# ConvFFN of a hybrid encoder layer: token passes reordered to 768, 768 and 576, feature tiles walked back and forth, operands reloaded in one transfer per product

## The chip, the core and the metric

The kernel runs on one core of a Trainium2 chip, in float32, with matrix operands split into a high and a low half (float32r). The metric is the device time of one execution in microseconds, as the median of several runs.

## What is computed

The kernel is one inference step of one layer for a prompt of 2048 tokens and a sample of 64 tokens. Its first part is token mixing (latent attention and gated linear attention). After it come the output projection with a gated residual, a second norm with modulation, and the gated ConvFFN, and these are what the change touches:

```python
x = x + mods[2][:, None, :] * mixed                 # mixed = concat(o_mla, o_gla) @ w_out
h = _modulate(x, p['g_norm2'], mods[3], mods[4])
a, g = jnp.split(h @ p['w_up'], 2, axis=-1)         # w_up (1024, 2*2816)
a_ext = jnp.concatenate([hist, a], axis=1)
conv = p['b_conv']
for j in range(3):
    conv = conv + p['w_conv'][j] * a_ext[:, j:j + L]
y = (jax.nn.gelu(conv) * g) @ p['w_down']           # w_down (2816, 1024)
return x + mods[5][:, None, :] * y, a_ext[:, L:]    # outputs, new convolution history
```

## The kernel before

**Stages.** Projections, gated linear attention and attention take the first 1431 us. Then 17 output tiles of 128 tokens (the last, tile 16, is the sample with 64) go through `out_tile` (L1050): transposes, 48 products with w_out, residual, norm, transposes, and the eight combinations in `comb` (L1084). The FFN follows from L1228 on.

**The up-product** is a seven-product scheme (Strassen-Winograd) on halves of the model dimension, of features against gates, and of token halves. `PRODUCTS` (L58) lists its seven products m with the combination s of `comb` that each uses. `h2[m]` holds a pair of tiles per product, the high half and the low half of that combination, for all tokens of a pass. Each product is 12 matmuls in three-term split form. An FFN step handles one tile of 128 features f (22 of them) for one token pass; `PASSES` (L55) are tiles 0 to 3 with the sample, 4 to 9, and 10 to 15. Hence 66 steps, numbered n. Each matmul of a product has 288 columns in pass 0 and 384 in passes 1 and 2.

**What a step does** is written out by hand in `slot` (L1253), where `at(t, fn)` puts an operation at a due time and all operations of PE, ACT, DVE and POOL are emitted in the order of their due times (L1512). A step has its seven products, the sums of banks (`keep`, `add_bank`, `sum_kept`), three convolution taps, gelu, the gating and the split of the result u into halves. In the gaps between products 5, 3, 7 and 4 and after them stand the down-products of the step before (`down_tile`, one per token tile, 6 matmuls of 512 columns), each with an addition to its accumulator `acc`. Beside that the step prepares the next step's weights: four block sums on POOL (`block_sum`), seven splits (high half on ACT, low half for 5, 6, 7 and 3 on POOL, for 1, 2 and 4 on DVE). The row weights `wd` are loaded and split in the step that uses them. All loads and stores are issued from SP's queue. Column weights are loaded two steps ahead (`load_next`) into four buffers `fst`.

**The turn** between two passes: tiles 4 to 15 store `comb` to `comb_d` in device memory (L1109), one tensor per tile, 8 KB runs per partition. In the last step of a pass, each product's operands are fetched in three pieces of two transfers (`fetch`, L1413) into four staging buffers `h2st`, then split into `h2` (`piece_hi` on ACT, `piece_lo` on DVE, the last piece on POOL). The down tiles of that step also finish the outputs: `residual` loads the x1 rows into two buffers `xs`, `gate_` multiplies the accumulator by the gate row (POOL for even tiles, DVE for odd ones, DVE for all at the end), `finish_` adds `xs` on DVE and stores y. Each of these is due a few us after its tile's products. At f = 0 an accumulator is copied from PSUM by ACT instead of added.

**The start.** `ffn_start` (L1183) frees the output projection's pools, loads the convolution rows, and at the last tile the column weights of steps 0 and 1 are loaded and those of step 0 summed and split (L1212 to L1225). `comb` has a single buffer.

Of the kernel before, what the change touches and what calls it, by code (L numbers as in the profile page):

```python
# [21 lines left out]
P = 128  # L22
# [32 lines left out]
PASSES = ((0, 4, True), (4, 6, False), (10, 6, False))  # L55
# [6 lines left out]
def kernel(  # L62
# [51 lines left out]
    comb_d = [dr.tile([P, 8, 4, 64], F32, tag=f"combd{t}", name=f"comb_d{t}") for t in range(4, NT)]  # L114
# [933 lines left out]
    gt, wk4, h2 = {}, None, {}  # L1048

    def out_tile(t, n, seq, src, pos0, tok0):  # L1050
# [4 lines left out]
        if t in (0, 4, NT):  # L1055
            gt[seq] = gate_rows(wk, 0, seq, "gate")
# [16 lines left out]
        yield "proj"  # L1073
        x1 = wk.tile([P, D], F32, tag="x1", name="x1", bufs=1)
# [4 lines left out]
        Q.dma_start(x1_d[tok0:tok0 + n], x1[:n])  # L1079
        xn = norm_rows(wk, x1, n)  # L1080
# [23 lines left out]
        if t < 4 or seq:  # L1104
            c0 = 64 * (4 if seq else t)
# [32 lines left out]
    hp = c5.enter_context(tc.tile_pool(name="hp", bufs=1, side="right"))  # L1138
# [7 lines left out]
    def gate_rows(pool, g, s, tag):  # L1146

        o = pool.tile([P, D], F32, tag=tag, name="gate", bufs=1)
# [5 lines left out]
    fw = fcol = hist = None  # L1154
# [7 lines left out]
    def load_cols(c0):  # L1162
        s = fw.tile([P, KD, P], F32, tag="fst", name="fst", bufs=4)
# [19 lines left out]
    def ffn_start():  # L1183
        nonlocal fw, fcol, hist
        c4.close()
        fw = c7.enter_context(tc.tile_pool(name="fw", bufs=1))
        fcol = fw.tile([P, 4, NF], F32, tag="fcol", name="fcol")
        hist = fw.tile([P, 2, NF], F32, tag="hist", name="hist")
        fr = fw.tile([4 * NF, P], F32, tag="sraw", name="fr", bufs=4)
        Q.dma_start(fr[:3 * NF], w_conv.rearrange("j (f p) -> (j f) p", p=P))  # L1190
        Q.dma_start(fr[3 * NF:], b_conv.rearrange("j (f p) -> (j f) p", p=P))
        fh = fw.tile([4 * NF, P], F32, tag="sraw", name="fh", bufs=4)
        Q.dma_start(fh[:2 * NF], state_ffn_conv.rearrange("j (f p) -> (j f) p", p=P))
        yield
# [5 lines left out]
    with ExitStack() as c6:  # L1200
        wk = wk4 = c6.enter_context(tc.tile_pool(name="wk4", bufs=2, side="right"))

        next(outs[0])
        for t in range(len(tiles) + 1):
            g = outs[t] if t < len(tiles) else iter(())
            prev = outs[t - 1] if t else iter(())
# [378 lines left out]
```

## Time and profile before

| | |
|---|---|
| median of 3 runs | 3227.69 us (3224.61 to 3233.64) |
| the profiled execution's own time | 3225.37 us |
| its span, first to last instruction | 3223.0 us |
| TensorE matmul busy | 3037.8 us, 94% of the span |
| weight loads / DVE / ACT / POOL busy | 2649.7 / 2495.6 / 1477.4 / 1430.2 us |
| mean granted TensorE clock | 0.968 of full speed |
| moved by DMA | 295 MB, mean 92 GB/s |

The busy shares are averages over stages with different limits. To read a stage, take the busy time of each engine in a stretch of it: the engine that is busy in the whole stretch sets its length, and where none is, a chain of waits does. The granted clock is 1.00 where TensorE runs at full speed. The chain of waits names, going back from the last instruction, what each step of the way waited for. All stretches in the FFN are cut where a step's first product starts.

### The profile page before, as it was taken

Reading aid. Unit: us, or ns where it says so; the run is one execution under the profiler, and the core shown is the slowest. Engines: PE = TensorE matmul, PEld = TensorE weight load, DVE = VectorE, ACT = ScalarE, POOL = GpSimd, SP = SyncE. Lnnn points to the kernel's source line nnn. Section 1 sums busy time; section 2 is a strip of 40 time slices with the busy share of each in tenths; the row PEclk is TensorE's granted clock in tenths of the full one; section 3 lists DMA queues with packets and bytes.
Section 4 is the critical chain, followed back from the end, with each engine's and each line's share of the span. In section 5 each row is a group of like instructions: output and inputs, shape, how many; then the busy total and the mean of one; then the engine's idle time right before and its main releaser. Section 6 shows DMA issues by size and latency. Waiting matters only on the chain.

```text
span 3223.0 us, 46980 instructions
## 1 busy us (share of the span) xinstructions
PE 3037.8 (94%) x16730; PEld 2649.7 (82%) x16730; DVE 2495.6 (77%) x4640; ACT 1477.4 (46%) x3211; POOL 1430.2 (44%) x1161
## 2 busy tenths in 40 slices
PE   8999999999899999999979999979999998999996
PEld 4999787888668888877858888869999987999995
DVE  4776788777788888865438999977787888778786
ACT  4655433333357777754325444444343443434341
POOL 0222222212232322103248888866666666666661
PEclk9999999999889999999989999989999999999998
DMA  7544521111121211113562322252222234222222
GB/s 255 158 132 121 144 76 59 50 56 43 61 69 48 66 44 54 33 38 125 202 212 74 91 79 82 89 186 66 72 61 78 59 115 144 68 70 65 73 61 85
DMA packets 296410, 295.34 MB, mean 92 GB/s; under 512 B 60727, under 2 KB 239751, under 8 KB 294639
## 3 DMA queue, kind: packets, MB, share of 16 engines
q1 hardware_dynamic: 296175, 292.34, 29.6%
q8 instruction: 131, 2.15, 0.3%
q14 instruction: 104, 0.85, 0.1%
HBM read 223.73 MB, written 68.55 MB: 91 GB/s over the span
## 4 chain that ended last, share of the span: by engine, by line
PE 40%; POOL 7%; DVE 5%; issue 4%; DMA 2%; ACT 1%; SPq 0%; POOLq 0%; ACTq 0%; DVEq 0%
PE bank L1272 19%; PE bank L1448 11%; PE bank L96 6%; POOL sraw L1176 3%; POOL wu L1344 3%; DVE acc L1459 1%; PE bank L876 1%; PE bank L863 1%; DVE wu L1344 1%; DVE acc L1481 1%; DMA xs<-x_d 1%; POOL m L1297 1%; DMA h2st<-comb_d 1%; DVE cv L1330 1%; ACT wu L1391 0%
## 5 line engine op out<-in xcount | busy, mean ns | idle before, releaser
L1272 PE MATMUL bank<-h,wu 128*128 128x384 f32 (+1 forms) x5544 | 960.0, 328 | 66.5 <-ACT m L1291 58.3
L1272 PEld LDWEIGHTS bank<-h,wu 128*128 128x128 f32 x5544 | 922.7, 191 | 103.7 <-ACT m L1291 71.8
L1448 PE MATMUL bank<-wd,u 128*128 128x512 f32 (+1 forms) x2244 | 573.1, 399 | 11.3 <-DVE wd L1344 8.5
L1344 POOL TENSOR_TENSOR wu<-sraw,wu 128x512 fp32r<-128x512 f32 x260 | 376.7, 1449 | 392.3 <-ACT wu L1391 390.9
L1448 PEld LDWEIGHTS bank<-wd,u 128*128 128x128 f32 (+1 forms) x2244 | 411.2, 187 | 99.0 <-DVE wd L1344 9.4
L1459 DVE TENSOR_TENSOR acc<-acc,bank 128x512 f32<-128x512 f32 (+1 forms) x714 | 451.3, 678 | 47.2 <-PE bank L1448 42.8
L96 PE MATMUL bank<-w_g,hs 128*128 128x512 f32 (+4 forms) x1632 | 319.8, 346 | 0.0
L1344 DVE TENSOR_TENSOR wu<-fst,wu 128x512 fp32r<-128x512 f32 x195 | 234.2, 1227 | 96.3 <-ACT wu L1391 95.6
L96 PEld LDWEIGHTS bank<-w_g,hs 128*128 128x128 f32 (+1 forms) x1632 | 249.2, 187 | 33.9 <-issue 2.5
L91 DVE TENSOR_TENSOR pp<-bank,pp 128x512 fp32r<-128x512 f32 (+5 forms) x344 | 196.0, 576 | 37.3 <-ACT pp L88 32.7
L876 PE MATMUL bank<-pp,vv 128*128 128x512 f32 (+5 forms) x688 | 209.8, 391 | 13.0 <-DVE ob L900 6.7
L851 ACT ACTIVATE pr<-bank,mx 128x512 f32<-128x512 f32 (+4 forms) x328 | 204.7, 629 | 30.5 <-DVE mx L844 21.1
L1330 DVE SCALAR_TENSOR_TENSOR cv<-a_sb,fcol,cv 128x768 f32<-128x768 f32 (+1 forms) x132 | 212.0, 1606 | 5.1 <-ACT cv L1326 2.9
L88 ACT CAST pp<-bank 128x512 fp32r<-128x512 f32 (+5 forms) x344 | 170.0, 504 | 97.7 <-PE bank L863 95.2
L839 DVE TENSOR_REDUCE mx<-bank 128x1 f32<-128x512 f32 (+4 forms) x328 | 194.9, 599 | 24.5 <-PE bank L838 18.6
L1391 ACT CAST wu<-sraw 128x512 fp32r<-128x512 f32 x260 | 159.6, 614 | 97.1 <-POOL sraw L1176 59.7
L96 PE MATMUL bank<-w_o,mT 128*128 128x512 f32 (+1 forms) x816 | 199.0, 400 | 3.7 <-ACT mT L88 3.2
L96 PEld LDWEIGHTS bank<-w_o,mT 128*128 128x128 f32 (+1 forms) x816 | 149.8, 187 | 46.6 <-DVE mT L91 6.7
L1297 POOL TENSOR_TENSOR m<-m,m 128x384 f32<-128x384 f32 (+1 forms) x132 | 168.4, 1276 | 42.3 <-ACT m L1291 37.2
L1176 POOL TENSOR_TENSOR sraw<-fst 128x512 f32<-128x512 f32 x132 | 184.9, 1401 | 2.3 <-DMA fst<-w_up 2.3
L863 PE MATMUL bank<-ident,pr 128*128 128x128 f32 (+1 forms) x1112 | 178.0, 275 | 3.3 <-DVE pp L91 2.2
L1326 ACT ACTIVATE cv<-a_sb,fcol 128x768 f32<-128x768 f32 (+1 forms) x66 | 64.7, 981 | 243.0 <-DVE a_sb L1314 237.5
(254 smaller groups left out, 5197.1 us busy)
## 6 DMA issues: line engine op xcount, KB each, us to landing
fst<-w_up SPq DMA_DIRECT2D x132, 512.0 KB
fst<-w_down SPq DMA_DIRECT2D x66, 512.0 KB
x<-x_prompt SPq DMA_DIRECT2D x32, 512.0 KB
ada_w<-w_ada SPq DMA_DIRECT2D x64, 256.0 KB
comb_d<-comb SPq DMA_DIRECT2D x12, 1024.0 KB
h2st<-comb_d SPq DMA_DIRECT2D x84, 128.0 KB
wst<-w_ada SPq DMA_DIRECT2D x16, 512.0 KB
hT_d<-hT SPq DMA_DIRECT2D x16, 512.0 KB
```

The lines of the kernel that those rows point to most:

```text
L91: (lo_eng or V).tensor_tensor(lo, src, hi.bitcast(F32), op=ALU.subtract)
L96: T.matmul(out, a, b, start=first and i == 0, stop=last and i == 2)
L851: S.activation(pr[:qn, :b - a], box["s", i, j][:qn, :b - a], AF.Exp, bias=nb, accum_out=ls[:qn, i, j:j + 1])
L863: T.transpose(pt[:kn, i * qn:(i + 1) * qn], pr[:qn, j * P - a:j * P - a + kn], ident[:qn, :qn])
L876: T.matmul(box["o"][:, cs_], vv[:kn, key0 // P + j, :], pp[i][:kn, cs_], start=j == 0 and i == 0, stop=j == nk - 1 and i == 1)
L1176: G.tensor_tensor(s, x, y, op=op)
L1272: T.matmul(b[:, :cols_], w[m][i][:, k], h2[m][j][:, k, :cols_], start=first and k + i + j == 0, stop=k == 3 and i == 1, skip_group_check=n ...
L1297: G.tensor_tensor(o[a][:, :cols_], o[a][:, :cols_], o[b][:, :cols_], op=ALU.add)
L1330: V.scalar_tensor_tensor(v, o["a"][:, j:j + tot], col(j), v, op0=ALU.mult, op1=ALU.add)
L1344: eng.tensor_tensor(out[1], src, out[0].bitcast(F32), op=ALU.subtract)
L1448: T.matmul(po[c][:rows_], o["u"][a][:, c0:c0 + rows_], o["wd"][b][:, c * 512:(c + 1) * 512], start=a + b == 0, stop=a == 1)
L1459: V.tensor_tensor(x, x, y, op=ALU.add)
```

## The change

- `PASSES` becomes tiles 0 to 5, tiles 6 to 11, and tiles 12 to 15 with the sample: 768, 768 and 576 tokens. Output tiles run in their natural order 0 to 16, tiles 0 to 5 are split into `h2` at once, and 6 to 16 are stored.
- `comb_d` is one tensor per later pass, in the layout of `h2`. A tile's store then consists of 32 runs of 256 bytes per partition.
- The reload at a turn is one transfer per product straight into the low half's tile `h2[m][1]`; the high half is cast from it in two halves by ACT, the low half is subtracted in place in two halves, on POOL for products 5, 6 and 7 and on DVE for the others.
- Pass 1 walks the feature tiles from 21 down to 0, so the first step of a pass has the f of the step before it. That step reuses the column weights `w` (`w_next = w`) and the row weights (`wd_kept`): no loads, sums and splits for it.
- The finals of a turn: the gate multiplication is in halves and on DVE, the final addition on POOL, and their due times are 5.5 us per tile apart, from 1.6 us after the first down tile. In the last step the final addition is on DVE for odd tiles and on POOL for even ones, and due times stay.
- Accumulators are a ring of eight buffers in a pool of their own, opened in step 0.
- `out_tile` has one more `yield`, after the residual. The convolution rows are loaded and transposed at tile 4, step 0's column weights are loaded at tile 13, and after tile 16's residual they are summed and split, before tile 15's last part. Tile 16's norm and combinations are put into FFN step 0, at 0.1 and 7.5 us.
- The pools around the FFN get `reuse_waits="tile"`, by its name a wait per tile for the memory of a closed pool.

```diff
-PASSES = ((0, 4, True), (4, 6, False), (10, 6, False))
+PASSES = ((0, 6, False), (6, 6, False), (12, 4, True))
...
-    comb_d = [dr.tile([P, 8, 4, 64], F32, tag=f"combd{t}", name=f"comb_d{t}") for t in range(4, NT)]
+    comb_d = [dr.tile([P, 8, 4, 64 * nt + 32 * smp], F32, tag=f"combd{t}", name=f"comb_d{t}") for t, nt, smp in PASSES[1:]]
...
         yield "proj"
+        wk = wk4b
...
         Q.dma_start(x1_d[tok0:tok0 + n], x1[:n])
+        yield "res"
         xn = norm_rows(wk, x1, n)
...
-            Q.dma_start(comb_d[t - 4], comb)
+            Q.dma_start(comb_d[p - 1][:, :, :, c0:c0 + hn], comb[:, :, :, :hn])
...
-    otiles = tiles[:4] + tiles[NT:] + tiles[4:NT]
-    outs = [out_tile(*ti) for ti in otiles]
+    outs = [out_tile(*ti) for ti in tiles]
...
-    hp = c5.enter_context(tc.tile_pool(name="hp", bufs=1, side="right"))
+    hp = c5.enter_context(tc.tile_pool(name="hp", bufs=1, side="right", reuse_waits="tile"))
+    fc = c5.enter_context(tc.tile_pool(name="fc", bufs=1, side="right", reuse_waits="tile"))
...
+        if t == 4:
+            conv_rows(w0)
+        if t == len(tiles) - 4:
+            raws = [{"a": load_cols(0, w0, 2), "g": load_cols(FF, w0, 2)}]
+        next(prev, None)
+        next(prev, None)
+        if t == len(tiles) - 1:
+            next(g)
+            c6a.close()
+            c4.close()
+            fw = c7.enter_context(tc.tile_pool(name="fw", bufs=1, reuse_waits="tile"))
+            raws.append({"a": load_cols(P), "g": load_cols(FF + P)})
+            for m in (5, 6, 7, 3):
+                block_sum(raws[0], m)
+            w_f = {}
+            for m, s in PRODUCTS:
+                w_f[m] = two(f"wu{m}_")
+                split(*w_f[m], block(raws[0], m), lo_eng=G if m in (3, 5, 6, 7) else V)
+        next(nxt, None)
+        next(prev, None)
...
-        steps = [(p, f) for p in range(len(PASSES)) for f in range(NF)]
+        steps = [(p, f if p % 2 == 0 else NF - 1 - f) for p in range(len(PASSES)) for f in range(NF)]
...
+            if first_f and n:
+                at(base + 2, rows_kept)
+            else:
+                at(base + 2, rows)
+                at(after + 1.0, rows_hi)
+                at(after + 2.5, lambda: lo(o["wd"], o["sd"], V))
...
+            if raw is None:
+                w_next = w
...
-            if f == NF - 1 and p + 1 < len(PASSES):
+            if last_f and p + 1 < len(PASSES):
+                w1 = 64 * PASSES[p + 1][1] + 32 * PASSES[p + 1][2]
+                there = base
+
+                def fetch(m, s):
+                    moving(m)
+                    Q.dma_start(h2[m][1].bitcast(F32)[:, :, :w1], comb_d[p][:, s])
+
+                def half_hi(m, ks):
+                    S.copy(h2[m][0][:, ks, :w1], h2[m][1].bitcast(F32)[:, ks, :w1])
+
+                def half_lo(m, ks, eng):
+                    h, l = h2[m][0][:, ks, :w1], h2[m][1][:, ks, :w1]
+                    eng.tensor_tensor(l, l.bitcast(F32), h.bitcast(F32), op=ALU.subtract)
+
                 for m, s in PRODUCTS:
...
+                    there = max(there, end[m]) + 3.3
+                    at(end[m] + .1, fetch, m, s)
+                    for i in range(2):
+                        ks, eng = slice(2 * i, 2 * i + 2), G if m in (5, 6, 7) else V
+                        at(there + 1.5 + i, half_hi, m, ks)
+                        at(there + 2.6 + (2.0 if eng is G else 1.2) * i, half_lo, m, ks, eng)
...
+                    if first_f:
+                        acc[i] = ac.tile([P, D], F32, tag="acc", name="acc", bufs=8)
...
+                    late = o.setdefault("late", t) + 5.5 * i + 1.6
...
-                        V.tensor_tensor(a, a, o["xs", i, c][:rows_], op=ALU.add)
+                        (V if last and i % 2 else G).tensor_tensor(a, a, o["xs", i, c][:rows_], op=ALU.add)
...
+                        at(t - 1.5 + c * .5 if last else late - 4 + c, residual, c)
+                        at(t + 1.4 + c * .1 if last else late + 2.5 * c, gate_, c)
+                        at(t + 2.5 + c * .1 if last else late + 1 + 2.5 * c, finish_, c)
...
+        raws += [{} if n % NF else None for n in range(2, len(steps))] + [None] * 2
...
+        at(.1, next, outs[-1])
+        at(7.5, next, outs[-1])
+        at(13.0, open_acc)
```

## Rows read from the trace of the kernel before

**Rows 1.** Timeline of TensorE: start us, us, engine line op tiles xcount [idle before <-releaser]

```profile
1647.34 11.63 PE L96 MATMUL bank<-w_o,mT 128*128 128x512 f32 x48
...
1692.37 6.13 PE L1272 MATMUL bank<-h,wu 128*128 128x288 f32 x24 [13.52 <-ACT m L1291]
...
2099.70 3.25 PE L1272 MATMUL bank<-h,wu 128*128 128x288 f32 x12 [9.80 <-ACT m L1291]
```

**Rows 2.** Windows, by stage: stretch, its us, each engine's busy us, clock, DMA

```profile
core 0: us, PE busy (x) PEld busy (x) DVE busy (x) ACT busy (x) POOL busy (x), PEclk, DMA share, GB/s
1593.30:1606.43 13.13, 13.13 (x67) 10.66 (x65) 5.89 (x12) 3.87 (x8) 3.87 (x5) 1.00 0.54 201
1658.97:1704.85 45.88, 20.32 (x102) 18.35 (x101) 14.59 (x29) 15.16 (x30) 25.80 (x25) 0.67 0.56 185
1704.85:1725.22 20.37, 18.71 (x116) 16.46 (x115) 17.29 (x23) 13.62 (x28) 18.71 (x17) 1.00 0.27 78
1968.00:1986.84 18.84, 18.63 (x117) 16.46 (x116) 18.70 (x28) 8.30 (x17) 15.84 (x13) 1.00 0.29 85
2081.93:2179.81 97.88, 73.48 (x350) 65.62 (x348) 78.12 (x96) 43.27 (x78) 69.67 (x48) 0.86 0.53 164
2226.30:2249.55 23.25, 23.25 (x122) 21.60 (x120) 18.50 (x26) 9.30 (x16) 14.32 (x12) 1.00 0.23 68
2621.49:2719.41 97.92, 78.39 (x362) 70.04 (x360) 86.29 (x95) 43.66 (x77) 67.95 (x43) 0.90 0.52 164
3161.09:3184.30 23.21, 23.21 (x121) 21.41 (x119) 14.61 (x23) 5.55 (x9) 3.28 (x3) 1.00 0.00 1
3184.30:3223.00 38.70, 9.64 (x39) 6.67 (x38) 25.87 (x36) 1.60 (x2) 0.00 (x0) 0.71 0.48 150
```

**Rows 3.** Chain of waits: start us, us, what; issue to landing where DMA

```profile
1432.33 2.01 DMA mix_d<-ob
...
1674.10 8.81 DMA comb_d<-comb
...
1687.92 3.82 DMA comb_d<-comb
...
3192.12 1.34 DMA conv_prompt<-ob
...
3196.61 3.92 DMA xs<-x_d
```

**Rows 4.** Timeline: one width on DVE without and with POOL beside, and on POOL

```profile
1692.86 0.69 DVE L1344 TENSOR_TENSOR wu<-fst,wu 128x512 fp32r<-128x512 f32 x1 [0.73 <-ACT wu L1391]
...
1937.00 1.77 DVE L1344 TENSOR_TENSOR wu<-fst,wu 128x512 fp32r<-128x512 f32 x1
...
2232.56 1.29 POOL L1176 TENSOR_TENSOR sraw<-fst 128x512 f32<-128x512 f32 x1
```

**Rows 5.** Timeline of FFN steps: undisturbed operations, and the first down-product of a step

```profile
2182.56 1.22 DVE L1344 TENSOR_TENSOR wd<-fst,wd 128x1024 fp32r<-128x1024 f32 x1
...
2188.29 1.55 PE L1448 MATMUL bank<-wd,u 128*128 128x512 f32 x6
...
3175.66 2.07 DVE L1330 SCALAR_TENSOR_TENSOR cv<-a_sb,fcol,cv 128x768 f32<-128x768 f32 x2
...
3177.36 2.35 POOL L1297 TENSOR_TENSOR m<-m,m 128x384 f32<-128x384 f32 x2 [17.65 <-ACT m L1291]
...
3179.79 1.01 POOL L1337 TENSOR_TENSOR cv<-cv,m 128x384 f32<-128x384 f32 x1
...
3184.12 0.83 ACT L1341 CAST u<-cv 128x768 fp32r<-128x768 f32 x1 [5.51 <-PE bank L1448]
...
3185.51 0.95 DVE L1348 TENSOR_TENSOR u<-cv,u 128x768 fp32r<-128x768 f32 x1
```

**Rows 6.** Timeline of two output tiles: a comb store's issue, the next tile's first write

```profile
1601.56 0.32 SPq L1109 DMA_DIRECT2D comb_d<-comb  x1
...
1608.94 0.40 DVE L1098 TENSOR_SCALAR comb<-bank,mod_a,mod_b 128x128 f32<-128x128 f32 x1
```

More of the change, by code (lines that the diff above doesn't have):

```diff
@@ L1144, with gate_rows @@
         moving(m)
-    def gate_rows(pool, g, s, tag):
-        o = pool.tile([P, D], F32, tag=tag, name="gate", bufs=1)
+    def gate_rows(pool, g, s, tag, bufs=1):
+        o = pool.tile([P, D], F32, tag=tag, name="gate", bufs=bufs)
         Q.dma_start(o, gate_d[g, s:s + 1].partition_broadcast(P))
@@ L1198, in ffn_start @@
             V.tensor_copy(dst.rearrange("p j f -> p (j f)"), pt[:, :n])
[L1200 to L1206, printed above, removed]
-            nxt = outs[t + 1] if t + 1 < len(tiles) else iter(())
-            next(nxt, None)
-            next(g, None)
-            if t == 0:
-                next(g)
-            if t == len(tiles) - 1:
-                start = ffn_start()
-                next(start)
-                raws = [{"a": load_cols(i * P), "g": load_cols(FF + i * P)} for i in range(2)]
-                for m in (5, 6, 7, 3):
-                    block_sum(raws[0], m)
-            next(prev, None)
-            next(nxt, None)
-            if t == len(tiles):
-                run(start)
-                w_f = {}
-                for m, s in PRODUCTS:
-                    w_f[m] = two(f"wu{m}_")
-                    split(*w_f[m], block(raws[0], m), lo_eng=G if m in (3, 5, 6, 7) else V)
-            next(prev, None)
@@ L1228 @@
-    with ExitStack() as c8:
-        wk = c8.enter_context(tc.tile_pool(name="wk5", bufs=1))
+    c6, c6a = ctx.enter_context(ExitStack()), ctx.enter_context(ExitStack())
+    w0 = c6.enter_context(tc.tile_pool(name="w0", bufs=1, side="right", reuse_waits="tile"))
+    wk4b = c6.enter_context(tc.tile_pool(name="wk4b", bufs=1, side="right", reuse_waits="tile"))
+    wk = wk4 = c6a.enter_context(tc.tile_pool(name="wk4", bufs=2, side="right", reuse_waits="tile"))
+    next(outs[0])
+    for t in range(len(tiles)):
+        g = outs[t]
+        prev = outs[t - 1] if t else iter(())
+        nxt = outs[t + 1] if t + 1 < len(tiles) else iter(())
+        next(nxt, None)
+        next(g, None)
+        if t == 0:
+            next(g)
[6 more added lines that the diff above has]
+        if t == len(tiles) - 1:
+            next(g)
+            c6a.close()
[8 more added lines that the diff above has]
+                split(*w_f[m], block(raws[0], m), lo_eng=G if m in (3, 5, 6, 7) else V)
+        next(nxt, None)
+        next(prev, None)
@@ L1399, in slot @@
             if raw_next is not None:
-                g_ = (f + 2) % NF
+                g_ = steps[n + 2][1]
                 def load_next(k):
@@ L1441, in products @@
                 def products():
-                    if f == 0 and i == 0:
-                        acc.clear()
-                        acc.extend(wk.tile([P, D], F32, tag=f"acc{j}", name=f"acc{j}") for j in range(nt + smp))
+                    if first_f:
+                        acc[i] = ac.tile([P, D], F32, tag="acc", name="acc", bufs=8)
                     o["po", i] = po = [bank(), bank()]
```

96 lines of the change are left out of this document (40 added, 56 removed).

## The prediction

> **What bounds the kernel now.** I read the chain of waits first, then cut the span where it changes character, at the starts of FFN steps. A step is one feature tile f of one pass: 84 up-products, among them the down-products of the step before. Step numbers n run 0 to 65; a turn is the three steps around a change of pass, and E is the end of the last output projection, at 1658.97 us [rows 1]. The stretches in [rows 2] add up to the time from E to the end:
>
> - start, steps 0 and 1: 45.88 + 20.37 = 66.3
> - steps 2 to 20, small pass: from 1725.22 to 2081.93, 356.7 (18.8 each)
> - turn 1, steps 21 to 23: 97.9
> - steps 24 to 42, large pass: 441.7 (23.25 each)
> - turn 2, steps 43 to 45: 97.9
> - steps 46 to 65: from 2719.41 to 3184.30, 464.9
> - tail: 38.7
>
> The sum is 1564.0, and 1658.97 + 1564.0 = 3223.0, the span. A large step is TensorE's own: PE is busy in all of its 23.25 us, DVE in 18.50, POOL in 14.32. A small step is not: DVE is busy 18.70 of 18.84. The output projection tiles too are PE's, 13.13 of 13.13. So time can only be won at the start, the two turns and the tail, where PE is busy 20.3 of 45.9, 73.5 and 78.4 of 97.9, and 9.6 of 38.7 [rows 2]; there the granted clock also falls to 0.67, 0.86, 0.90 and 0.71.
>
> What holds PE there? At the start PE is idle 13.52 us [rows 1]: the last tile's `comb` waits for its single buffer, whose store was issued at 1674.10 behind the FFN's loads and took 8.81 us instead of 3.82 [rows 3]. ACT's copies for step 0 queue behind that `comb`. In the turns PE idles up to 9.80 us for ACT copies [rows 1] that queue behind reloaded pieces. Under that lies a second bound. A 128x512 DVE op with both inputs in SBUF takes 0.69 us with POOL idle and 1.77 beside POOL work; the same width on POOL takes 1.29 [rows 4]. If such DVE work and all POOL work are added at undisturbed lengths [rows 4, 5], a large step has on DVE 2.07 (taps) + 3x0.69 + 1.22 + 0.95 + 0.48 (half of 0.95, estimated) = 6.8, and on POOL 8x1.29 + 2.35 + 1.01 = 13.7, together 20.5. Scaling its token-wide terms by 578/768 gives 18.8 for a small step, which takes 18.84. Turn 2 has 3x20.5, reload splits 14x0.69 + 7x1.29 = 18.7, gates 6x1.29 + 3x1.22 = 11.4 and finals 12x0.69 = 8.3: 99.8, and takes 97.9. Turn 1 gives 95.5 in the same way, and takes 97.9. So I use this side-by-side sum as the turn's limit. It is a regularity of these four stretches, not a law.
>
> **The change part by part.** *Start.* Tile order becomes 0 to 16, pass 0 needs tiles 0 to 5 only, and E does not move: tile count and widths are the same. Step 0's column weights are loaded three tiles early, and their sums and splits go into space that w_o releases row by row if the tile-wise reuse does what its name says; the conv rows move to tile 4. That puts 4 sums and 4 POOL splits (8x1.29 = 10.3) beside a projection during which POOL is busy only 3.87 of 13.13 [rows 2]. Splits that are not done by E lie under the first products. The last tile's norm is cut in two and moved into step 0, so nothing of it stands before product 1. On PE's path I count 1 us of transposes for tile 15, 2 for a first split that comes late, 14.8 for the up-products (by columns, 84x384 of the 84x384 + 36x512 that make up 23.25) and 0.6 for tile 16's transposes: 18.4, taken as 19. In step 1 POOL is still late: 10.3 for step 0, eight `comb` sums of half that width or less (about 5) and a step's own 13.7 make 29 from about E - 7, and the first down-product of step 1 is due 8.5 us into it, at E + 27.5. I add 4 for that. Together 19 + 23.25 + 4 = 46. The bounds are 40 (no wait) and 74 (today's 66.3 plus 8 because both steps are now large).
>
> *comb store.* Eleven tiles store `comb` in 256-byte pieces, 4096 of them, instead of 128 long ones. The `comb` buffer is single: the store is issued 7.38 us before the next tile's first write (1601.56 to 1608.94) [rows 6]. 22 KB took 1.34 us and 128 KB in 256-byte pieces 2.01 [rows 3], so 8 x 0.67 + 1.34 = 6.7 us is my estimate; it just fits, and I count 0. The lower bound is 3.82, today's long store; the upper 8x2.01 = 16.1. The Trainium skill (DMA: Bandwidth & Descriptors, Specifications) speaks against this edit: it puts line rate at pieces of 512 bytes or more, with a read-modify-write below. By the row the sum stays; by the page the store is slower than a long one by a factor that it doesn't give, which is the slower rival below.
>
> *Reload.* 42 transfers per turn become 7 of 768 KB (576 KB at turn 2), written straight into the low halves' tile. At the rate of the 1 MB store (3.82, of it 1.34 fixed) [rows 3] 768 KB take 3.2, and the code spaces them at 3.3 us, each behind its product. By the code's due times each split is done 7 us or more before its product in the next step, so a transfer may take about 4 us without harm. Behind a late one ACT queues with its bank copies (in order, as today); 14 half casts at 0.83 [rows 5] are 11.6 on an ACT that is busy 9.30 of 23.25. On SP the fetches stand before the column loads for two steps later, which have a step to spare.
>
> *Turn 1* is now three large steps: 61.4. It loses one step's column preparation (8x1.29 + 3x0.69 = 12.4) and one row split (1.2). Reload splits are 8x0.95 on DVE and 6x1.94 (1.5x1.29) on POOL = 19.2, half a us more than today. Gates are all on DVE (12x0.69 = 8.3), and finals move from DVE to POOL, 12x1.29 = 15.5 instead of 8.3. Sum 90.8 against PE's 3x23.25 = 69.8: 21 over. Of these 4.5 are free, since a step's last split ends at 2183.78 and its first down-product starts at 2188.29 [rows 5], and the next step repays 23.25 - 20.5 = 2.8. I take 14: turn 1 = 83.8. Bounds for the excess: 3 (the spread finals fill idle port time) and 28, today's.
>
> *Turn 2* is one large and two small steps: 20.5 + 2x18.8 - 12.4 - 1.2 + 8x0.71 + 6x1.45 + 8.3 + 15.5 = 82.6, against 23.25 + 2x18.84 and one more down tile (6x0.232 in the code) = 62.3. Of 20 over, 4.5 are free; a small step repays nothing. POOL now waits for `xs` (load 3.92 [rows 3] + 1.29 in each of two buffers, tiles 5.5 apart: just enough), for which I add 1.5. Excess 17, bounds 5 and 35: turn 2 = 79.3.
>
> *Steady steps.* 19 + 19 large at 23.25 are 883.5, 20 small at 18.84 are 376.8. The small pass has a two-column copy from `halo` in place of a memset, not counted.
>
> *Tail.* Ten loads through two buffers, a pair per tile (3.92 + 0.69 each), become eight: -4.6; POOL's even tiles cost 3 x 0.6 more. 38.7 - 3.2 = 35.5; bounds 33 and 40 (a gate row waits in SP's queue).
>
> **Sum.** 46 + 441.7 + 83.8 + 441.7 + 79.3 + 376.8 + 35.5 = 1504.8, against 1564.0: -59. The profiled execution took 3225.4 (span 3223.0) and would take 3166; the median of the runs is 2.3 above the profiled one, so 3168.
>
> **The rivals.** *Turns stay as long as today*: a reload slower than 4 us stalls ACT in order, or POOL waiting for `xs` stalls the sums behind it. For it: the store that took 8.81 among other loads [rows 3]. Against: 7 transfers need no staging buffer. Excess 28 and 35 instead of 14 and 17: 3168 + 32 = 3200. *The start stays*: the new pool waits for all of w_o, or POOL's backlog holds products 6 and 5. Then 74 instead of 46: 3196. *The port sum doesn't hold when work is spread*: excess 3 and 5, start 42: about 3141. *Slower*: the 256-byte store paces the output projection. From a landing of 7.38 us on, each further us delays the next `comb`, nine times (tiles 6 to 15). At 16.1 a tile takes 8.7 more: 78 in all, 3246. The page named above points this way. It beats the gains from a landing of 14 us, which the 2.01 row at its worst reading allows. *The change doesn't do what it says*: kept weights still wait for a reload, and the turns gain nothing; that falls together with the first rival.
>
> **How the numbers follow.** Forecast 0.57 (3155 to 3182); turns stay 0.11; start stays 0.12; port sum fails 0.12; slow store 0.06; none of these, within noise of today 0.02. 0.3% is about what a measurement of this kernel tells from no change, 10 us: faster means below 3218. Faster 0.90, same 0.04 (half-slow stores, or both gains lost), slower 0.06. The range runs from the port rival to the two stay rivals, 3138 to 3202.
>
> **What would show it.** Right: PE idle under 5 us after E; step 1 starting near E + 19; DVE two-input ops at 1.8 us and POOL near full in the turns; small steps at 18.8 at the end. Wrong: `comb` waiting for its DMA in the output tiles, ACT waiting for `comb_d` reloads, turns at 70 (the port sum is no limit) or at 98.

## The result, and the profile after

The changed kernel takes 3176.32 us (median of 4, 3170.42 to 3178.98), the kernel before in the same comparison 3228.95 (median of 4, 3224.61 to 3233.64): a ratio of 0.9834, 95% interval 0.9814 to 0.9854. The prediction was 3168 with a range of 3138 to 3202. The total is 8 us off. Several of its terms missed by more, in both directions.

Windows by stage of the kernel after (columns as in [rows 2]): output tiles, step 0, step 1, steps 2 to 20, turn 1 (steps 21 to 23), step 24, turn 2 (steps 43 to 45), step 46, the small steps 47 to 65 without the last one's end, one small step, and the tail.

```profile
1439.62:1664.15 224.53, 223.18 (x1078) 177.39 (x1078) 113.01 (x202) 77.62 (x172) 76.55 (x98) 1.00 0.59 163
1664.15:1701.34 37.19, 21.44 (x101) 19.54 (x100) 21.79 (x24) 13.15 (x26) 23.71 (x23) 0.77 0.57 139
1701.34:1724.96 23.62, 23.38 (x122) 21.46 (x121) 13.62 (x16) 15.18 (x28) 20.98 (x15) 1.00 0.32 99
1724.96:2165.00 440.04, 440.04 (x2282) 409.24 (x2280) 349.73 (x473) 177.96 (x288) 271.41 (x208) 1.00 0.24 69
2165.00:2248.07 83.07, 74.50 (x362) 67.06 (x360) 75.69 (x79) 36.70 (x61) 63.87 (x37) 0.96 0.49 163
2248.07:2275.58 27.51, 23.71 (x122) 21.39 (x120) 22.62 (x26) 10.80 (x20) 25.37 (x20) 1.00 0.37 113
...
2693.06:2770.43 77.37, 67.04 (x355) 60.26 (x354) 71.30 (x87) 33.10 (x62) 58.48 (x40) 0.91 0.51 154
2770.43:2793.92 23.49, 20.06 (x116) 17.72 (x114) 20.15 (x27) 9.46 (x19) 22.70 (x19) 0.93 0.51 162
2793.92:3139.80 345.88, 345.88 (x2167) 314.12 (x2165) 338.48 (x513) 159.08 (x298) 279.99 (x220) 1.00 0.28 81
...
2921.37:2939.57 18.20, 18.20 (x115) 16.54 (x114) 18.06 (x28) 8.57 (x16) 15.40 (x13) 1.00 0.29 88
...
3139.80:3173.60 33.80, 8.18 (x33) 5.22 (x32) 19.83 (x30) 1.53 (x2) 8.48 (x6) 0.72 0.42 126
```

Against [rows 2]: step 0 takes 37.2 instead of 45.9, at a granted clock of 0.77 instead of 0.67; the two turns of 97.9 are 83.1 and 77.4, but steps 24 and 46 now take 27.5 and 23.5, more than the steps after them; and a small step takes 18.20 with PE busy in all of it, where before it took 18.84 with PE waiting. Term by term, in us:

| stretch | predicted | measured | difference |
|---|---|---|---|
| start to the end of the output projection | 1658.97 | 1664.15 | +5.2 |
| steps 0 and 1 | 46 | 60.8 | +14.8 |
| steps 2 to 20 | 441.7 | 440.0 | -1.7 |
| turn 1 | 83.8 | 83.1 | -0.7 |
| steps 24 to 42 | 441.7 | 445.0 | +3.3 |
| turn 2 | 79.3 | 77.4 | -1.9 |
| steps 46 to 65 | 376.8 | 369.4 | -7.4 |
| tail | 35.5 | 33.8 | -1.7 |

They add up to 3173.7, the span of the profiled execution (3173.6 us, its own time 3175.5), 9.9 above the predicted sum.

**The first 1440 us are the same code and scatter.** The first transpose of the output tiles came at 1431.7 in the kernel before and at 1439.6 after. In the three profiled executions that have the old code behind that point it came at 1431.7, 1437.6 and 1442.1, in the eleven that have the new code, the experiments among them, at 1436.5 to 1446.5. So 8 us of difference there prove nothing about the change. From that transpose on, the profiled kernel before took 3223.0 - 1431.7 = 1791.3 and the one after 1734.0, 57.3 less, against 59 predicted. For the same reason the runs below are compared by stretches that begin with an FFN step, not by their totals.

**The stall that stayed.** Timeline of the kernel after in step 0 (start us, us, engine line op tiles [idle before <-releaser]):

```profile
1671.80 7.52 DVE L261 TENSOR_SCALAR xn<-x,r 64x1024 f32<-64x1024 f32 x1
...
1680.41 1.18 POOL L1105 TENSOR_TENSOR comb<-comb 128x256 f32<-128x256 f32 x1
...
1681.62 11.34 SPq L1112 DMA_DIRECT2D comb_d<-comb  x2
...
1688.23 0.34 DVE L1100 TENSOR_SCALAR comb<-bank,mod_a,mod_b 128x64 f32<-128x64 f32 x1 [6.09 <-DMA comb_d<-comb]
...
1690.89 0.47 ACT L1306 COPY m<-bank 128x384 f32<-128x384 f32 x1
...
1691.41 7.15 PE L1287 MATMUL bank<-h,wu 128*128 128x384 f32 x24 [11.26 <-ACT m L1306]
```

This is the mechanism of [rows 1, 3] again. Tile 15's last `comb` sum ends at 1681.6 on a POOL that is full with step 0's and step 1's sums and splits; only then is its store issued; tile 16's first write of the same buffer waits for it on DVE until 1688.2; ACT's writes alternate with DVE's; and ACT's copy of a product of step 0 (L1306) comes behind them on ACT, at 1690.9. PE waits 11.26 us, 2.3 less than the 13.52 of before. Of the eleven `comb` stores it is the only one that anything waits for, as the view of line 1112 says:

```profile
who waited for it (us, times):
  DVE comb L1100: 6.1, 1
```

### The profile page after: what moved, and what is told of

Read it like the earlier page. It is cut to its first block, busy times and chain, and to the rows that moved or that the text cites. A ratio compares the mean times of both kernels' runs of the same rounds, so it can differ in the third digit from the quotient of the medians.

```text
span 3173.6 us, 46762 instructions
## 1 busy us (share of the span) xinstructions
PE 3028.5 (95%) x16730; PEld 2650.4 (84%) x16730; DVE 2479.6 (78%) x4617; ACT 1472.2 (46%) x3188; POOL 1439.5 (45%) x1170
## 5 line engine op out<-in xcount | busy, mean ns | idle before, releaser
L1359 POOL TENSOR_TENSOR wu<-sraw,wu 128x512 fp32r<-128x512 f32 x252 | 365.4, 1450 | 347.0 <-ACT wu L1415 347.0
L1359 DVE TENSOR_TENSOR wu<-fst,wu 128x512 fp32r<-128x512 f32 x189 | 215.6, 1166 | 93.6 <-ACT wu L1415 92.0
L839 DVE TENSOR_REDUCE mx<-bank 128x1 f32<-128x512 f32 (+4 forms) x328 | 194.9, 599 | 24.4 <-PE bank L838 18.4
L1415 ACT CAST wu<-sraw 128x512 fp32r<-128x512 f32 x252 | 154.9, 615 | 80.9 <-PE bank L1287 47.3
L863 PEld LDWEIGHTS bank<-ident,pr 128*128 128x128 f32 (+1 forms) x1112 | 135.9, 141 | 39.9 <-DVE pp L91 9.3
```

Source lines behind the costliest of these rows:

```text
L839: V.reduce_max(mx[:qn, c:c + 1], po[:qn, :b - a], axis=AX.X)
L863: T.transpose(pt[:kn, i * qn:(i + 1) * qn], pr[:qn, j * P - a:j * P - a + kn], ident[:qn, :qn])
L1359: eng.tensor_tensor(out[1], src, out[0].bitcast(F32), op=ALU.subtract)
```

## Experiments

Times of steps run from a step's first up-product to the next step's. The total of a single execution includes the scatter above, so the text reads stretches. These scatter too: in the four executions that share the code of the turns (the kernel after, e1, e5 and e10) steps 21 to 24 take 110.3 to 110.7 us and steps 43 to 47 take 117.9 to 119.1.

### The start: is it the queue or POOL's backlog?

**e1_late16**

```diff
-        at(7.5, next, outs[-1])
-        at(13.0, open_acc)
+        at(22.0, next, outs[-1])
+        at(27.0, open_acc)
```

> Edit: the last output tile's comb part moves from 7.5 to 22 us into step 0 by the due times, and the opening of the accumulators' space from 13 to 27. Queue theory: the 11.3 us in which PE waited for ACT's copy of product 1 (step 0 took 36.6) came from ACT and DVE standing in order at the last tile's comb writes, which wait for the store of the tile before. Then PE's hole after the first products goes, step 0 falls to 24 to 28, steps 0 and 1 together from 60.8 after the end of the output projection to 48 to 53, and the whole by 8 to 12 us. Rival, POOL's backlog: POOL is busy without a gap from 1674.1 to 1683.3 with step 0's sums and splits, and these hold products 6, 5 and 7 whatever comb does; then step 0 stays at 33 or more. Second rival, the hole only moves: the comb writes stand in the queue ahead of step 1's copies instead, and step 1 grows from 23.6 by 5 or more.

Measured: step 0 took 23.8 instead of 36.6, step 1 27.7 instead of 23.6, together 51.5 instead of 60.2 (52.1 instead of 60.8 from the end of the output projection). Windows of steps 0 and 1, and TensorE's timeline:

```profile
1667.87:1691.64 23.77, 18.45 (x95) 16.53 (x93) 20.18 (x19) 11.92 (x22) 20.83 (x18) 0.93 0.63 164
1691.64:1719.33 27.69, 25.08 (x123) 23.14 (x121) 14.00 (x20) 16.41 (x32) 23.62 (x20) 0.94 0.48 126
```

```profile
1669.01 2.03 PE L1287 MATMUL bank<-h,wu 128*128 128x384 f32 x10 [0.55 <-DVE wu L91]
...
1672.98 0.62 PE L1287 MATMUL bank<-h,wu 128*128 128x384 f32 x2 [1.94 <-ACT wu L88]
...
1683.11 4.49 PE L1287 MATMUL bank<-h,wu 128*128 128x384 f32 x24 [0.98 <-ACT m L1306]
...
1698.75 6.03 PE L1287 MATMUL bank<-h,wu 128*128 128x384 f32 x24 [2.61 <-ACT m L1306]
```

The 11.26 us hole became 0.98, though POOL is fuller than before (20.83 of 23.77, where it was 23.71 of 37.19). So the queue was the cause and POOL's backlog alone was not. The edit also moves the opening of the accumulators' space, but the wait that went is the one that the trace puts down to the `comb` writes. A part of the second rival holds too: these writes now stand ahead of step 1's copies and cost 2.61 there. The net is 8.7 us.

### The turns: is the side-by-side sum a limit?

With a large step behind turn 1 and two small ones behind turn 2 the prediction's side-by-side sum is 90.8 + 20.5 = 111.3 and 82.6 + 2 x 18.8 = 120.2; measured are 110.6 (steps 21 to 24) and 119.1 (steps 43 to 47). For the whole it fits. If it were a limit, every edit of the work would move the turns by its own length.

**e2_finals_dve**

```diff
-(V if last and i % 2 else G).tensor_tensor(a, a, o["xs", i, c][:rows_], op=ALU.add)
+(V if not last or i % 2 else G).tensor_tensor(a, a, o["xs", i, c][:rows_], op=ALU.add)
```

> Edit: in the two turns the additions of the finals (12 of 128x512 in turn 1, 12 in turn 2) go back from POOL to DVE; nothing else moves. Side-by-side sum (the prediction's tool): an addition costs 0.69 on DVE instead of 1.29 on POOL, so 12 x 0.6 = 7.2 us come off each turn: turn 1 with step 24 from 110.6 to about 103.4, turn 2 with step 46 from 100.9 to about 93.7. Rival, DVE's own queue is the bound: DVE is busy in 75.7 of turn 1's 83.1 us already; with 12 more operations of 0.69 to 1.77 it would need 84 to 97, so the turns stay or grow by up to 14. Rival, neither: unchanged within 1 us.

**e3_lo_dve**

```diff
-ks, eng = slice(2 * i, 2 * i + 2), G if m in (5, 6, 7) else V
+ks, eng = slice(2 * i, 2 * i + 2), V
```

> Edit: all 14 low halves of the reloaded operand on DVE; so far 6 of them per turn (blocks 5, 6, 7; 128x768) are POOL's. Side-by-side sum: 0.95 on DVE instead of 1.85 to 1.94 on POOL, so 6 x 0.95 = 5.7 us off turn 1 (110.6 with step 24 to 105) and 6 x 0.7 = 4 off turn 2 (100.9 with step 46 to 97). Rival, DVE's own queue: POOL's six lie beside other work and DVE gets six more in the step before the pass change, ahead of the taps; the turns grow by 3 to 9. Rival, neither: unchanged within 1 us.

**e4_reload**

```diff
-raws += [{} if n % NF else None for n in range(2, len(steps))] + [None] * 2
+raws += [{} for n in range(2, len(steps))] + [None] * 2
...
-            if first_f and n:
-                at(base + 2, rows_kept)
-            else:
-                at(base + 2, rows)
+            at(base + 2, rows)
```

> Edit: at the first step of a pass the column and row operands are loaded, summed and split again, as in every other step, instead of being kept; the passes still walk back and forth. Side-by-side sum: each turn gets 4 sums and 4 low halves on POOL at 1.28, 3 low halves on DVE at 0.69 and one row split at 1.22 back, 13.6 us together: turn 1 with step 24 from 110.6 to about 124, turn 2 with step 46 from 100.9 to about 114, the whole plus 27. Rival, the turns are held by something else (the order in which splits, taps and finals queue, or the transfers): the turns grow by 5 or less each, though DVE's and POOL's busy times grow by 13 and more.

**e7_nofinals**

```diff
-V.tensor_tensor(a, a, o["gate", i][:rows_, cc], op=ALU.mult)
+if last:
+    V.tensor_tensor(a, a, o["gate", i][:rows_, cc], op=ALU.mult)
...
-(V if last and i % 2 else G).tensor_tensor(a, a, o["xs", i, c][:rows_], op=ALU.add)
+if last:
+    (V if i % 2 else G).tensor_tensor(a, a, o["xs", i, c][:rows_], op=ALU.add)
```

> Left out: in the two turns the multiplication by the gate (12 of 128x512 on DVE each) and the addition of the residual (12 on POOL each); loads and stores stay, so the rows of the first two passes are the raw sums. Side-by-side sum: 12 x 0.69 + 12 x 1.29 = 23.8 us of work goes from each turn, more than the excess over PE's time (17.8 and 21.6): turn 1 with step 24 falls from 110.6 to PE's 4 x 23.2 = 93, steps 43 to 47 from 119.1 to 98 to 100. Rival, work costs only part of its length in a turn, as the operand preparation did when it was put back (5.4 and 5.9 us instead of 13.6): the turns fall by 9 to 10 and an excess of 8 to 12 stays, which the reload then owns.

**e8_nolo**

```diff
-at(there + 2.6 + (2.0 if eng is G else 1.2) * i, half_lo, m, ks, eng)
```

> Left out: the low halves of the reloaded operand in both turns (8 operations of 128x768 on DVE, 6 on POOL per turn, 19.2 us at undisturbed lengths); the transfers and the high halves on ACT stay, so the products of the last two passes are off. Without the finals, step 22 still took 29.96 instead of 23.2 and step 44 27.76 instead of about 19.8, so about 7 to 8 us of each turn's excess lie in the first step after the pass change. Theory, the splits' work on DVE and POOL owns them: step 22 falls to 24 to 26, turn 1 with step 24 from 110.6 to 101 to 104, steps 43 to 47 from 119.1 to 110 to 113. Rival, the transfers or ACT's casts own them: step 22 stays at 29 or more and the turns stay within 2 us.

**e9_nospread**

```diff
-at(t - 1.5 + c * .5 if last else late - 4 + c, residual, c)
-at(t + 1.4 + c * .1 if last else late + 2.5 * c, gate_, c)
-at(t + 2.5 + c * .1 if last else late + 1 + 2.5 * c, finish_, c)
+at(t - 1.5 + c * .5, residual, c)
+at(t + 1.4 + c * .1, gate_, c)
+at(t + (2.5 if last else 4) + c * .1, finish_, c)
```

> Edit: in the turns the finals get the due times they had in the kernel before (residual 1.5 us before a tile's last down-product, gate 1.4 after it, addition 4 after it) instead of one tile each 5.5 us; the engines stay as they are (gate on DVE, addition on POOL). Side-by-side sum: the same work in the same turn, so turn 1 with step 24 stays at 110.6 and steps 43 to 47 at 119.1, within 2 us. Rival, spreading is a gain of its own: the gates and additions crowd into the step after the pass change ahead of step work, DVE and POOL hold ACT's and PE's banks, and each turn grows by 5 to 10. Rival, spreading costs: the additions were late only because they wait for their due time, and each turn shrinks by 2 to 5.

Measured, in us, beside what the sum makes of each edit (where PE's own time is longer, 4 x 23.2 = 92.8 and 62.3 + 2 x 18.2 = 98.7, that stands). The sum's entries for e3, e8 and turn 2 use the prediction's lengths, 0.95 and 1.94 for a large and 0.71 and 1.45 for a small half:

| kernel | steps 21 to 24: sum | measured | steps 43 to 47: sum | measured |
|---|---|---|---|---|
| after | 111.3 | 110.6 | 120.2 | 119.1 |
| e2, additions on DVE | 104.1 | 114.5 | 113.0 | 120.1 |
| e3, low halves on DVE | 105.4 | 112.1 | 115.8 | 120.5 |
| e4, operands loaded again | 124.9 | 115.9 | 133.8 | 125.0 |
| e7, no gates and additions | 92.8 | 99.8 | 98.7 | 105.6 |
| e8, no low halves | 92.8 | 102.0 | 105.8 | 113.0 |
| e9, finals not spread | 111.3 | 118.4 | 120.2 | 127.3 |

The sum misses all six edits. Putting 13.6 us of work back (e4) costs 5.4 and 5.9; taking 23.8 out (e7) gains 10.8 and 13.5; moving work from POOL to the engine where it is shorter (e2, e3) loses 1.0 to 4.0 where 4.4 to 7.2 should be gained (of these losses only e2's 4.0 in turn 1 is far above the scatter; the gains are missing in all four); and moving no work at all (e9) costs 7.8 and 8.2. What stands instead is read from the steps. Windows of steps 22 and 23 of the kernel after, of step 23 in e2, of steps 22 and 23 in e7 and in e8, and of step 23 in e9:

```profile
2189.49:2219.99 30.50, 25.80 (x122) 22.78 (x120) 30.43 (x31) 11.82 (x19) 27.61 (x16) 0.94 0.22 70
2219.99:2248.07 28.08, 25.26 (x122) 22.81 (x120) 27.21 (x26) 12.19 (x24) 26.38 (x17) 0.94 0.53 171
```

```profile
2223.78:2259.23 35.45, 25.71 (x121) 23.07 (x120) 31.58 (x39) 13.24 (x25) 18.49 (x12) 0.90 0.52 163
```

```profile
2186.47:2216.44 29.97, 25.81 (x122) 22.79 (x121) 29.31 (x32) 12.04 (x20) 27.59 (x16) 0.94 0.31 99
2216.44:2239.59 23.15, 23.15 (x121) 21.53 (x120) 11.22 (x16) 13.37 (x25) 14.05 (x12) 1.00 0.31 101
```

```profile
2190.89:2214.08 23.19, 23.19 (x121) 21.56 (x120) 17.98 (x23) 11.81 (x19) 14.26 (x11) 1.00 0.29 92
2214.08:2241.78 27.70, 23.73 (x121) 21.40 (x120) 26.79 (x26) 12.24 (x24) 26.14 (x16) 1.00 0.57 173
```

```profile
2222.03:2262.41 40.38, 28.82 (x121) 25.91 (x120) 25.48 (x28) 13.24 (x25) 33.09 (x24) 0.79 0.51 156
```

Step 22 belongs to the reload: DVE is busy in 30.43 of its 30.50 us, and without the low halves (e8) the step takes PE's 23.19 with DVE at 17.98. Part of DVE's busy time may be POOL's doing: single low halves of 128x768 take DVE 1.76 to 2.40 us in this turn beside POOL's work, where an operation of that size takes 0.95 undisturbed [rows 5]. e8 drops the halves of both engines, so their shares are not separated. Steps 23 and 24 belong to the finals: without them (e7) both take 23.16, and step 22 stays at 29.97. The two shares, 10.8 for the finals and 8.6 for the low halves, together are a little more than turn 1's excess of 17.8 over PE's time. An edit counts only until its step falls to PE's 23.2; that is why e7 and e8 gain less than the work they drop. Part of what e4 adds lies in step 21, which has idle time: its step 21 takes 25.1, only 0.6 more than without. e3 gives the full DVE of step 22 six more low halves and makes that step 32.31, against 30.39 to 31.70 in the five executions that share it (the kernel after, e1, e5, e10 and e11). e2 loses in step 23.

In e2's step 23 (35.45) and e9's (40.38) no engine is full: DVE 31.58 and 25.48, POOL 18.49 and 33.09. A chain of waits holds them. It starts at a load of `xs`, first in e2, then in e9:

```profile
2246.89 0.69 DVE L1505 TENSOR_TENSOR acc<-acc,xs 128x512 f32<-128x512 f32 x1 [3.36 <-DMA xs<-x_d]
...
2248.14 1.03 ACT L1341 ACTIVATE cv<-a_sb,fcol 128x768 f32<-128x768 f32 x1 [10.77 <-DVE a_sb L1329]
...
2251.07 4.10 PE L1287 MATMUL bank<-h,wu 128*128 128x384 f32 x12 [7.57 <-ACT m L1306]
```

```profile
2244.84 1.29 POOL L1505 TENSOR_TENSOR acc<-acc,xs 128x512 f32<-128x512 f32 x1 [4.58 <-DMA xs<-x_d]
...
2252.84 0.62 ACT L1415 CAST wu<-sraw 128x512 fp32r<-128x512 f32 x1 [6.58 <-POOL sraw L1181]
...
2253.89 4.21 PE L1287 MATMUL bank<-h,wu 128*128 128x384 f32 x12 [5.00 <-ACT m L1306]
```

An addition waits for its rows, which come through two buffers. Behind it on the same engine stands work of the step: `a_sb` on DVE in e2, the weight sums on POOL in e9. ACT waits for that work, and PE for ACT's copy of a product. In the kernel after, POOL waits only 0.2 us for `xs` in all of turn 1. So the trace gives a reason why spreading pays: the rows have come when the addition is due. The prediction's first rival had named this wait. No run gives `xs` more buffers in a turn, so it is read from the traces and not tested.

**e11_mix** asks whether POOL's share of the excess can be taken away alone: it is e10_tail (below) with the additions of the last two tiles of a turn on DVE.

```diff
-(V if last and i % 2 else G).tensor_tensor(a, a, o["xs", i, c][:rows_], op=ALU.add)
+(V if (i % 2 if last else i > 3) else G).tensor_tensor(a, a, o["xs", i, c][:rows_], op=ALU.add)
```

> Edit: e10_tail, and in the turns the additions of tiles 4 and 5 (4 of 12) on DVE, the other 8 on POOL. All 12 on DVE made step 24 5 us shorter than in the changed kernel (23.1 instead of 27.5) and step 23 7 us longer (35.5 instead of 28.1). Theory: the excess of steps 24 and 46 is POOL's (busy 25.4 of 27.5 and 22.7 of 23.5), that of the steps before it DVE's; taking 5 us from POOL's end alone gives step 24 back 3 to 5 us and step 46 1 to 3 at no cost to step 23: 5 us under e10_tail. Rival, DVE's queue: each addition delays the accumulation that PE's banks wait for; steps 23 or 24 grow as much as POOL gains, within 2 us of e10_tail.

Measured: 3160.71 us, ratio to the kernel before 0.9768 (0.9749 to 0.9787), the same as e10_tail. Step 24 falls to 23.2 from e10's 25.9, step 23 grows to 34.7 from 28.5; steps 21 to 24 take 112.2 against 110.7. The rival's outcome holds: what POOL's end gains is lost a step earlier. DVE is not full there (29.51 of 34.69); as in e2 its additions wait for `xs`, 3.30 and 1.78 us, and PE then waits 6.59 for ACT.

### The small steps: one state or two?

**e5_kick**

```diff
-        G.tensor_tensor(s, x, y, op=op)
+        for _ in range(1 + (extra.get(now[0], 0) if n in (7, 3) else 0)):
+            G.tensor_tensor(s, x, y, op=op)      # extra = {51: 1, 55: 2, 60: 4}
```

> Edit: in three steps of the last pass POOL computes two of the four weight sums again, once each in step 51 (2 operations of 1.28 us more), twice in step 55 (4 more), four times in step 60 (8 more); the values don't change. The last pass of the changed kernel runs at 18.21 us a step (PE busy in all of it), the small steps of the kernel before at 18.84 (DVE busy 18.70). Two-state theory: both are steady states of the same work, told apart by how far POOL lags DVE when DVE reaches the row split; a kick of 2.6 to 10 us pushes the step over, and after at least one of the kicks the steps stay at 18.8. One-state theory: POOL is busy only 15.4 of 18.2 and DVE 18.06 of 18.21, so a kick costs its own excess once and the steps are back at 18.21 two to five steps later; then the 18.84 of the kernel before comes from something in its code.

Measured: step 52 took 18.90, step 55 21.53 and step 60 29.01; each step behind them was back at 18.2. By this run alone the changed kernel has one state.

**e6_relief** (an edit of the kernel before)

```diff
-at(late, lambda m=m, g=g: lo(w_next[m], block(raw, m), G if g else V))
+if n == 9 and g or n == 15 and m != 4:
+    at(late, lambda m=m: S.copy(w_next[m][1], block(raw, m)))
+else:
+    at(late, lambda m=m, g=g: lo(w_next[m], block(raw, m), G if g else V))
```

> The kernel before, with part of the computation replaced: in step 9 the four low halves of weight blocks that POOL computes, and in step 15 those four and two of DVE's three, are written by ACT as plain copies (wrong values; 0.62 us each on ACT). POOL so gains 4 x 1.3 us in step 9, POOL 4 x 1.3 and DVE 2 x 0.7 to 1.8 in step 15. Two-state theory: after one of the two the small steps run at 18.2 instead of 18.84 to the end of the pass, 5 to 11 steps, so the pass is 3 to 7 us shorter. One-state theory: steps are back at 18.8 within two steps; 18.84 is what that code takes.

Measured: steps 4 to 8 at 18.83, step 9 18.24, steps 10 to 16 at 18.09 to 18.17, step 17 18.73, then 18.8 again. The first edit throws the code into the shorter step, and shortly after the second it is back. Whether the shorter one decays by itself is left open by this run, so the second edit was taken out.

**e12_relief9**

```diff
-if n == 9 and g or n == 15 and m != 4:
+if n == 9 and g:
```

> The kernel before, with the four low halves that POOL computes in step 9 written by ACT as plain copies (wrong values), and nothing else: the edit of step 15 that e6_relief had beside it is left away. There steps 10 to 16 took 18.17 us with POOL's first weight sum 0.1 us ahead of the step's first product, and from step 17 on, after the second edit, 18.84 again with that sum 1.55 us into the step. Two-state theory: each state holds itself, and it was the edit of step 15 that threw the code back; now all of steps 10 to 20 take 18.17, 7.4 us less for the eleven. Rival, the faster state decays by itself: from step 16 or 17 on the steps take 18.8 again.

Measured: all of steps 10 to 20 take 18.17. Windows of step 8 and step 14, then POOL's and DVE's timelines in the same two steps:

```profile
1846.40:1865.24 18.84, 18.37 (x115) 16.34 (x114) 18.70 (x28) 8.25 (x16) 15.85 (x13) 1.00 0.29 84
1956.19:1974.36 18.17, 18.17 (x116) 16.48 (x114) 18.03 (x28) 8.58 (x16) 15.44 (x13) 1.00 0.30 88
```

```profile
1847.97 1.30 POOL L1176 TENSOR_TENSOR sraw<-fst 128x512 f32<-128x512 f32 x1
1849.35 1.76 POOL L1176 TENSOR_TENSOR sraw<-sraw,fst 128x512 f32<-128x512 f32 x1
...
1956.08 1.30 POOL L1176 TENSOR_TENSOR sraw<-fst 128x512 f32<-128x512 f32 x1
1957.46 1.30 POOL L1176 TENSOR_TENSOR sraw<-sraw,fst 128x512 f32<-128x512 f32 x1
...
1849.88 2.32 DVE L1344 TENSOR_TENSOR wd<-fst,wd 128x1024 fp32r<-128x1024 f32 x1
1852.12 1.77 DVE L1344 TENSOR_TENSOR wu<-fst,wu 128x512 fp32r<-128x512 f32 x1
...
1959.36 1.21 DVE L1344 TENSOR_TENSOR wd<-fst,wd 128x1024 fp32r<-128x1024 f32 x1
1960.50 0.67 DVE L1344 TENSOR_TENSOR wu<-fst,wu 128x512 fp32r<-128x512 f32 x1
```

The same instructions, steady in two ways. In the longer step POOL's first sum starts 1.6 us behind the step's first product (1847.97 against 1846.40), its second lies beside DVE's row split, and that split takes 2.32. In the shorter one the first sum starts 0.1 us ahead (1956.08 against 1956.19), both are done before the row split, and that takes 1.21 and the next split 0.67 instead of 1.77. The work that POOL was spared lay in one step; eleven steps ran shorter. The shorter order does not hold from every start: in the three executions with the old code step 2 takes 18.17 and step 3 18.5 to 18.6, and then come steps of 18.8. The last pass of the changed kernel has the shorter order from step 47 on (in the step shown above POOL's first sum starts at 2921.23, 0.14 ahead of the first product, and the row split takes 1.21), and three kicks did not keep it out. In e1, e2, e4, e7, e8 and e11 one or two steps of 18.6 to 18.9 come up in that pass by themselves, and the next are back at 18.2. Why its code falls back into it while the code before settled in the longer one is not settled: the two differ in a halo copy, pools and waits.

### The tail

**e10_tail** (with e1's late tile 16)

```diff
+if last and i < nt:
+    if c == 0:
+        x = fw.tile([P, D], F32, tag="fst", name="xs", bufs=4)
+        Q.dma_start(x, x1_d[tile_ * P:tile_ * P + P])
+        o["xs", i, 0], o["xs", i, 1] = x[:, :512], x[:, 512:]
+    return
...
-at(t - 1.5 + c * .5 if last else late - 4 + c, residual, c)
+at(base + 8 + 2 * i + c * .5 if last else late - 4 + c, residual, c)
```

> Edit: the last output tile's comb part late as in e1_late16, and in the last step the residual rows of the four prompt tiles come in one transfer of 512 KB each into the four weight buffers that nothing loads any more, issued 8 to 14 us into the last step instead of 512-column halves through two buffers. Theory: the tail's chain was load, add, load, add through two buffers (36% of the last 34.7 us lie in these loads); with the rows there, the last accumulation is followed by gate, addition and store alone, the time from step 65's first product to the end falls from 52.0 to 43 to 46, and the whole kernel comes to 3158 to 3164, about 0.981 of the kernel before. Rival, DVE's queue holds the tail: it has the accumulations, the gates and half of the additions, and the gain is 3 us or less: 3167 to 3170.

Measured: 3160.21 us (median of 4, 3158.24 to 3168.82), ratio to the kernel before 0.977 (0.9753 to 0.9787; the kernel before took 3238.19 there, median of 7). The interval lies below that of the changed kernel (0.9814 to 0.9854): this version beats both. From step 65's first product to the end it takes 47.3, the changed kernel 52.0. The nine executions that share the changed kernel's tail (the kernel after, e1 to e5 and e7 to e9) take 52.0 to 54.9 there, so the gain is 4.6 to 7.5 us, more than the rival's 3 and mostly short of the 6 to 9 of the theory. e11, with the same tail as e10, takes 46.4. Chain of waits at the end of the kernel after (start us, us, what), then of e10_tail (there L1506 is the gate and L1511 the addition):

```profile
3156.54 3.75 DMA xs<-x_d
...
3160.42 1.78 POOL acc L1505
...
3162.22 3.12 DMA xs<-x_d
```

```profile
3146.52 1.19 DVE acc L1478 x2
3147.71 0.60 DVE acc L1506
3148.31 0.60 DVE acc L1511
...
3150.20 1.64 POOL acc L1511
```

The loads are out of the chain, and what they covered has come up: DVE's accumulations, gates and additions in one queue.

## Why the prediction came out as it did

- **Total and sign**: right. The predicted gain from the first output tile on was 59, measured 57.3, but partly by terms that cancel.
- **Start**: the step that failed is "cut in two and moved into step 0, so nothing of it stands before product 1". It holds for PE's own instructions: step 0's first product comes 0.6 us after the end of the projection, where it came 7.2 after. But on ACT and DVE tile 16's `comb` writes, which wait for tile 15's store, stood before the copies that free PE's banks. The prediction named this cause for the kernel before [rows 3] and did not follow it to the new place. From the end of the projection step 0 took 37.2 against 19. Step 1 took 23.6 against 27.25, so the 4 us for POOL in it were not needed. e1 shows the cause: with those writes late, the two steps take 52.1. Of the 6.1 still above 46, 5.4 lie in step 0, which takes 24.4 against 19: PE is busy 18.5 us there, at a granted clock of 0.93, where 15.4 had been added up, and waits 5.3, where 2 had been allowed for a late split.
- **The output stage**: the end of the last projection was forecast unmoved, with no change in the tiles. From the first transpose to that end it takes 224.5 instead of 227.3, and to step 0's first product 225.1 to 225.3 in the eleven executions with the new code against 234.1 to 235.7 with the old. That the end came 5.2 later is the scatter of the code ahead of it.
- **comb store**: right. No write of `comb` in the output tiles waits for a store. By the trace's packet records a 1 MB store in 256-byte pieces ends 6.1 to 6.3 us after its issue there, against an estimate of 6.7, and the next write comes 8.0 us after the issue (1593.89 to 1601.86). The store in step 0 took 6.6 until the write that waited for it. The long stores of the kernel before end 3.5 us after their issue where nothing else delays them. The Trainium skill (DMA: Bandwidth & Descriptors, Specifications) puts line rate at 512 bytes or more; the trace agrees in direction, with a factor of about 1.8 between the two kinds of store.
- **Turns**: 83.1 and 77.4 against 83.8 and 79.3, and 4.3 and 4.7 more in the step behind each than the 23.25 and 18.84 that the prediction gave them (it let step 24 repay 2.8). The reason was not right: the side-by-side sum fits the whole and fails for every edit, so that the turns came out so near is luck in part. It treated a turn as one pot of work. It is three or four steps, each with PE's time as its floor and with another engine or chain above it: the low halves with a full DVE in step 22, the finals in 23 and 24. The sign "ACT waiting for `comb_d` reloads" showed too, 4.4 us in turn 1, but PE waited only 1.05 in that step.
- **What the parts of the change were worth in the turns**: keeping the operands 5.4 and 5.9 (e4), spreading the finals 7.8 and 8.2 (e9). The sum had given the first 13.6 and the second nothing. No run puts back the old reload, the old pass sizes or the old place of step 0's weights, so what these were worth is not shown.
- **Small steps**: the term 20 x 18.84 was mis-sized; 19 of them take 18.21, 12.0 less, and step 46 4.7 more. The step taken over from the kernel before was one of two steady orders. The net 7.4 us hide half of the start's miss.
- **Tail**: 33.8 against 35.5, within the 3 us by which this stretch scatters, with the chain that was named: loads through two buffers.

## What to carry to other kernels

When an operation that waits for a DMA is moved, write down what stands behind it in the queue of every engine that it touches at the new place, not only what it no longer stands in front of. Here this held for `comb` at the start and, by the traces, for `xs` in the turns. Split a disturbed stretch into its steps, and ask for each which engine is busy in all of it and how far it can fall before TensorE's own time is the floor; a sum of work over the stretch can fit and still price no edit. A steady step is not a constant of the code: compare the order in which two engines meet in it before carrying its length over.

## What the runs showed of the hardware that was not expected

- One code has two steady step lengths, 18.84 and 18.17 us, and a relief of one step decided which for the next eleven (e12). A row split of 128x1024 on DVE takes 2.32 beside a POOL operation and 1.21 without.
- DVE's `xn` of 64x1024 took 7.52 us in step 0, and 7.48 to 7.52 in all eleven executions with the new code. The same operation, of the same size, took 0.73 to 0.74 in the three with the old code (first line, kernel before). In the kernel after it started at 1671.80, and beside it POOL ran seven operations one after the other, of 0.74 to 1.31 us (first and last of them); it ended 0.5 us after the seventh:

```profile
1506.04 0.73 DVE L261 TENSOR_SCALAR xn<-x,r 64x1024 f32<-64x1024 f32 x1
```

```profile
1671.67 1.28 POOL L91 TENSOR_TENSOR wu<-sraw,wu 128x512 fp32r<-128x512 f32 x1
...
1678.03 0.75 POOL L1103 TENSOR_TENSOR comb<-comb 128x256 f32<-128x256 f32 x1
```

  The Trainium skill (SBUF — State Buffer, Who interferes with whom) describes a port pair that the two engines hold exclusively for a whole instruction. The times fit a DVE that waits for that pair and lets seven holders pass, which is more than one instruction; that it was the port is a reading and not tested.
- Unchanged code before the output tiles ends anywhere in 1431.7 to 1446.5 us over fourteen profiled executions, 0.5% of the kernel and as much as many an edit here is worth.
